# A one-layer hybrid block on one core: h in spaced quarters, a layer norm in single-engine stages, own banks for four transposes, and another buffer for the gate bias

## The chip, the core and the metric

The program runs on one core of a Trainium2 chip. The metric is the time of one execution on the device in microseconds (us), as the median of several runs. Engines are called by their names or, in rows of the profile, by short ones: PE is TensorE (matmuls), PEld its loading of weights, DVE is VectorE, ACT is ScalarE, POOL is GpSimd, SP is SyncE. In this kernel POOL does almost nothing but issue transfers.

## The reference

One decoder layer (DEPTH 1, 256 positions, 2048 channels) with four parallel token mixers of width 1024, all in float32:

```python
h = rmsnorm(x, norm_g)
proj = einsum('bsd,df->bsf', h, w_in)                  # 2048 -> 18432, split into 14 parts
ya = stick_breaking_attention(a_q, a_k, a_v) * silu(a_g)
yb = conformer_conv(b_a, b_b, ...) * silu(b_g)         # GLU, 31-tap causal conv, layernorm over channels, silu
yc = spatial_gating(gelu(c_u), gelu(c_v), ...) * silu(c_g)
yd = dilated_mixture(d_q, d_k, d_v) * silu(d_g)        # 8 heads, 3 dilation groups
yproj = einsum('bsnc,ncd->bsnd', stack(ya, yb, yc, yd), w_branch)
gates = sigmoid(einsum('bsd,df->bsf', h, w_gate) + b_gate)   # one gate per branch and channel
merged = sum over branches of gates * yproj
out = rmsnorm(x + merged @ w_out, final_g)
```

The convolution's layer norm is: subtract the mean over the 1024 channels, divide by the root of the variance, scale and shift per channel, SiLU.

## The kernel before

**Jobs.** All weights stream from memory once, as 256 tiles of 128x2048 (1 MB). Nearly every tile is a job: SyncE loads it (st), ScalarE rounds it to float32r (hi, line 119), VectorE subtracts to get the remainder (lo, line 125), and TensorE multiplies with both parts (hi and lo of the weights against hi and lo of the activations, three products). A table of jobs (prog) is walked in order by run(): before job t's matmuls are issued, the load of job t+5 and the hi and lo of job t+2 are issued; behind the matmuls come the job's own post function and whatever earlier functions asked for with later(n, ...), "n jobs from now". The order of instructions on PE, ACT, DVE and SP is the order in which this Python code issues them; each engine works strictly in that order. GpSimd's order is set by the scheduler. There are three buffers each for hi and lo, six for st.

**Kinds of jobs.** In transposed projections (proj_t, mm_t: lines 261 and 264) the weights are stationary and a job is 16 matmuls of 512 columns and 16 of 256. In the others (mm_n: lines 313 to 315) the activations are stationary and a job is 24 matmuls of 512 columns; four jobs make a column of 512 outputs for two blocks of 128 positions (tb).

**PSUM.** Four pools of two banks: x, n, t and s. A column of mm_n takes the pair n or the pair t in turn (n_banks); a transposed projection takes one bank of t; small products of the mixers take s. The pair x is used for one column in the opening only.

**The stages, in order.** (1) Opening: 16 jobs make the values of d and a from x directly, while the statistics of h are taken (h_squares, h_rms) and h is made and split in four quarters (h_split, lines 241, 88, 89), each of which is four scalings on VectorE, a rounding on ScalarE and a subtraction on VectorE. h_rstd turns the root around for the values' scaling (d_out, a_out). (2) b's projections and its convolution on VectorE, then d's heads; head by head: scores, exponentials, softmax, transposes (pp), product with the values (o). The convolution's layer norm runs among the jobs of d's last two heads. (3) d's gates, b's gate path, branch d; b's gates; a's heads and c's units; gates and branches b, a, c in this manner: a gate column (gate_plain) adds its bias (bgb) on VectorE, ScalarE takes the sigmoid and stores it; a branch column (branch) multiplies the product by the gate (gl, line 491), adds the running sum from memory (ml, line 493) and stores it again. (4) In branch c the merged columns are transposed (turn, pt) and the output projection follows (pso).

**Buffers that the change touches.** The gate bias and the running sum share two buffers (pool sm2_p, tag ml). The values of the mixers (load_v) have one buffer (pool v_p, tag v). Both kinds of tile hold 2 KB in each partition. The bias of a column is loaded when the load of the column's first job is issued, five jobs ahead. In c's units, two mixing products (pz) of c's last two units stand behind the last matmul of c's first gate column; in the same way head 7's last product (o) stands behind that of d's first gate column. For branch b, yl (line 453) is the remainder of the branch's input.

Of the kernel before, what the change touches and what calls it, by code (L numbers as in the profile page):

```python
# [9 lines left out]
F32 = mybir.dt.float32  # L10
F32R = mybir.dt.float32r
AF = mybir.ActivationFunctionType
# [3 lines left out]
P = 128  # L16
# [34 lines left out]
C_K = 272  # L51
# [6 lines left out]
def hybrid_block(ctx: ExitStack, tc, w, x, xT, vec, bg, bgb, cst, dmask, sgu_wT, sgu_lg, sgu_lb, sgu_b, final_g, out):  # L58
    nc = tc.nc
    V, A, T = nc.vector, nc.scalar, nc.tensor  # L60
# [5 lines left out]
    v_p = ctx.enter_context(tc.tile_pool(name="v", bufs=1))  # L66
# [6 lines left out]
    sm2_p = ctx.enter_context(tc.tile_pool(name="ml", bufs=2))  # L73
    sm_p = ctx.enter_context(tc.tile_pool(name="sm", bufs=2))
    dr_p = ctx.enter_context(tc.tile_pool(name="dr", bufs=1, space=bass.MemoryType.DRAM))
    ps_x = ctx.enter_context(tc.tile_pool(name="psx", bufs=2, space=bass.MemoryType.PSUM))
    ps_n = ctx.enter_context(tc.tile_pool(name="psn", bufs=2, space=bass.MemoryType.PSUM))
    ps_t = ctx.enter_context(tc.tile_pool(name="pst", bufs=2, space=bass.MemoryType.PSUM))
# [8 lines left out]
    def split(hi, lo, src):  # L87
        A.activation(hi, src, AF.Copy)  # L88
        V.tensor_sub(lo, src, hi.bitcast(F32))
# [39 lines left out]
    def later(n, fn):  # L129

        t, left = now[0], n
        while left > 0 and t + 1 < len(prog):
            t += 1
            left -= prog[t].size
        calls.setdefault(max(t, now[0] + 1), []).append(fn)
# [8 lines left out]
    def put(job):  # L144
        prog.append(job)
# [25 lines left out]
    cst_sb = cp.tile([P, C_K], F32, name="cst_sb")  # L171
# [10 lines left out]
    def rsqrt(dst, src, n, shape):  # L182

        w = shape[1]
        sc = (so_p.tile([P, 2, w], F32, tag="so", name="rs") if w == S else
              ev_p.tile([P, 2, w], F32, tag=f"rs{w}", bufs=1, name="rs"))
        vp, sq = sc[:, 0, :], sc[:, 1, :]
        V.tensor_scalar(vp, src, 1.0 / n, EPS, op0=ALU.mult, op1=ALU.add)
        A.activation(sq, vp, AF.Sqrt)
        V.reciprocal(dst, sq)  # L190
        if shape[1] == 1:
            V.scalar_tensor_tensor(sq, dst, vp, dst, op0=ALU.mult, op1=ALU.mult)
        else:
            V.tensor_mul(sq, dst, dst)
            V.tensor_mul(sq, sq, vp)
        V.tensor_scalar(sq, sq, -0.5, 1.5, op0=ALU.mult, op1=ALU.add)
        V.tensor_mul(dst, dst, sq)
# [14 lines left out]
    def norm_g(k):  # L212
        return vec_sb[:, V_NG + k:V_NG + k + 1]
# [17 lines left out]
    def h_rms():  # L231
        red = box["red"]
        pst = ps_s.tile([P, 512], F32, tag="s", name="pst")
        T.matmul(pst[:, :S], ones, red[:, 0, :], start=True, stop=False)
        T.matmul(pst[:, :S], ones, red[:, 1, :], start=False, stop=True)
        rsqrt(rstd[:], pst[:, :S], float(D), [P, S])

    def h_split(q):
        for k in range(4 * q, 4 * q + 4):
            xk = xt[k // 8][:, k % 8, :]  # L240
            V.scalar_tensor_tensor(xk, xk, norm_g(k), rstd[:], op0=ALU.mult, op1=ALU.mult)
        ks = slice(4 * q, 4 * q + 4)
        split(xhl[:, ks, 0:S], xhl[:, ks, S:2 * S], xt[q // 2][:, 4 * (q % 2):4 * (q % 2) + 4, :])
# [7 lines left out]
    box = {}  # L251
# [53 lines left out]
    def mm_n(ps, weights, k0, lh, first, last, tbs=(0, 1)):  # L305

        hi, lo = weights
        for kk in range(4):
            o = kk * 512
            for tb in tbs:  # L310
                st = first and kk == 0
                sp = last and kk == 3
                T.matmul(ps[tb][:], lh(k0 + kk, 0, tb), hi[:, o:o + 512], start=st, stop=False)  # L313
                T.matmul(ps[tb][:], lh(k0 + kk, 0, tb), lo[:, o:o + 512], start=False, stop=False)  # L314
                T.matmul(ps[tb][:], lh(k0 + kk, 1, tb), hi[:, o:o + 512], start=False, stop=sp)  # L315

    def n_banks(i, name):

        pool, tag = ((ps_n, "n"), (ps_t, "t"))[i % 2]
        return [pool.tile([P, 512], F32, tag=tag, name=name) for _ in range(2)]  # L320
# [40 lines left out]
    def gate_plain(b, c):  # L361

        bi, acc = BRANCH[b], {}

        def fetch():
            acc["b"] = sm2_p.tile([P, 512], F32, tag="ml", name="bgb")
            o = c * 512
            nc.gpsimd.dma_start(acc["b"][:], bgb[bi, :, o:o + 512].to_broadcast([P, 512]))

        def mm(q):  # L370
            def fn(hi, lo):
                if q == 0:
                    acc["ps"] = n_banks(c, "psg")
                mm_n(acc["ps"], (hi, lo), 4 * q, x_lh, q == 0, q == 3)
            return fn

        def out_g():
            for tb in range(2):
                g = so_p.tile([P, 512], F32, tag="so", name="g")
                V.tensor_add(g[:], acc["ps"][tb][:], acc["b"][:])  # L380
                later(1, lambda tb=tb, g=g: out_s(tb, g))

        def out_s(tb, g):
            A.activation(g[:], g[:], AF.Sigmoid)
            nc.scalar.dma_start(g_dr[bi, tb, :, c * 512:(c + 1) * 512], g[:])
            stored.add((b, c, tb))

        for q in range(4):
            put(Job(("gateN", bi * 4 + c, q), mm(q), keep=(lambda st: fetch()) if q == 0 else None,
                    post=out_g if q == 3 else None))  # L390

    def v_plain(name, func, lh=None, pairs=None, scale=None, jobs=None):

# [36 lines left out]
    def put_y(b, h, n, src):  # L430
        nc.gpsimd.dma_start(y_dr[b][:, h:h + n, :], src)
        stored.update((b, "y", h + k) for k in range(n))
# [75 lines left out]
    def xu_banks(pool, tag):  # L508
        return lambda: [pool.tile([P, 512], F32, tag=tag, name="psv") for _ in range(2)]

    nc.gpsimd.dma_start(vec_sb[:, V_CW:], vec[:, V_CW:])
    d_out = v_plain("d_v", AF.Copy, xu_lh, (xu_banks(ps_n, "n"), xu_banks(ps_x, "x")), True, first_job)
    a_out = v_plain("a_v", AF.Copy, xu_lh, (xu_banks(ps_t, "t"), xu_banks(ps_n, "n")), True)
    at = {0: lambda: nc.sync.dma_start(cst_sb[:], cst[:, 0:C_K]), 3: h_squares, 5: lambda: (h_rms(), h_split(0)),
          6: lambda: h_split(1), 7: lambda: h_split(2), 8: lambda: h_split(3), 9: h_rstd,
          10: lambda: d_out(0), 11: lambda: d_out(1), 12: lambda: a_out(0), 15: lambda: later(1, lambda: a_out(1))}
    for i, fn in at.items():
        prog[i].post = fn

# [100 lines left out]
    def bc8(ap):  # L620
        return ap.unsqueeze(1).to_broadcast([P, KB, S])
# [6 lines left out]
    def chan_sum(red):  # L628
        ps = ps_s.tile([P, 512], F32, tag="s", name="pcs")
        T.matmul(ps[:, 0:S], ones, red[:], start=True, stop=True)  # L630
        return ps
# [6 lines left out]
    def conv_norm2(red):  # L638
        cv = box["cv"]
        pm = chan_sum(red)  # L640
        mean = sm_p.tile([P, S], F32, tag="mean", bufs=1, name="mean")
        A.activation(mean[:], pm[:, 0:S], AF.Copy, scale=1.0 / BW)
        V.tensor_sub(cv[:], cv[:], bc8(mean[:]))
        csq = s_p.tile([P, KB, S], F32, tag="s", name="csq")
        A.activation(csq[:], cv[:], AF.Square)
        later(2, lambda: conv_norm_r(csq))

    def conv_norm_r(csq):
        red = chan_red(csq[:])
        later(2, lambda: conv_norm3(red))  # L650

    def conv_norm3(red):
        cv = box["cv"]
        pv = chan_sum(red)
        rs = sm_p.tile([P, S], F32, tag="mean", bufs=1, name="rs")
        rsqrt(rs[:], pv[:, 0:S], float(BW), [P, S])
        V.tensor_mul(cv[:], cv[:], bc8(rs[:]))
        for i in range(8):
            A.activation(cv[:, i, :], cv[:, i, :], AF.Silu, bias=vec_sb[:, V_LB + i:V_LB + i + 1],
                         scale=vec_sb[:, V_LG + i:V_LG + i + 1])  # L660
        put_y("b", 0, KB, cv[:])

    for h0 in range(0, NH, 2):
# [24 lines left out]
    for c in range(4):  # L688
        gate_plain("d", c)
# [161 lines left out]
    mh, ml, held = [], [], {}  # L851

    def turn(c):
        if c == 0:
            mh.extend(s_p.tile([P, KB, S], F32R, tag="s", name=f"mh{i}") for i in range(2))
            ml.extend(s_p.tile([P, KB, S], F32R, tag="s", name=f"ml{i}") for i in range(2))
        for f0 in (0, 2):
            pt = ps_t.tile([P, 512], F32, tag="t", name="pt")
            for f in range(2):
                for tb in range(2):  # L860
                    o = f * S + tb * P
                    T.transpose(pt[:, o:o + P], held[c, tb][:, (f0 + f) * P:(f0 + f + 1) * P], ident)
            ks = slice(4 * (c % 2) + f0, 4 * (c % 2) + f0 + 2)
            src = pt[:].rearrange("p (f t) -> p f t", f=2)
            A.activation(mh[c // 2][:, ks, :], src, AF.Copy)
            V.tensor_sub(ml[c // 2][:, ks, :], src, mh[c // 2][:, ks, :].bitcast(F32))  # L866
# [46 lines left out]
    acc, wts = {}, {}  # L913
# [99 lines left out]
```

## Time and profile before

| | |
|---|---|
| median of 3 runs | 1512.89 us (1509.95 to 1514.67) |
| the profiled execution, its time | 1509.23 us |
| its span, first to last instruction | 1507.3 us |
| mean granted clock of TensorE | 0.995 |
| weight loads st in one transfer: number, size, median from issue to landing | 254, 1 MB, 4.9 us |
| DMA, mean over the span | 221 GB/s |

A row of the timeline reads: start, duration, engine, line, operation, what it writes and reads, shapes, how many were merged (x4), and in brackets how long the engine had been idle before it and what ended that. A row of a list of waits reads: who waited, for whom, us in total, how many times, the longest. A row of the view of windows reads: the stretch, its length, busy us and number of instructions (in brackets) of PE, PEld, DVE, ACT and POOL, then the granted clock of TensorE (1.00 is full), the busy share of the DMA engines and GB/s.

### The profile page before, as it was taken

How to read it: one execution, taken by the hardware profiler on the slowest of the kernel's cores; microseconds unless marked ns; L12 is line 12 of the kernel's file. 1: busy time of each engine (PE TensorE's matmuls, PEld its weight loads, DVE VectorE, ACT ScalarE, POOL GpSimd, SP SyncE). 2: the span in 40 equal slices, each digit the busy share in tenths (PEclk: the TensorE clock that was granted, in tenths of full speed). 3: DMA queues.
4: the chain of work that ended last, by engine and by line, in shares of the span. 5: the costliest groups of instructions: out<-in, count | busy, mean ns of one | idle time of the engine just before them, and what ended most of it. 6: DMA issues, size and time to landing. Idle time of an engine off the chain costs nothing.

```text
span 1507.3 us, 18226 instructions
## 1 busy us (share of the span) xinstructions
PE 1476.0 (98%) x7428; PEld 1248.4 (83%) x7428; DVE 946.2 (63%) x1080; ACT 704.2 (47%) x657; POOL 94.8 (6%) x174
## 2 busy tenths in 40 slices
PE   7999999999999899999999999999999999999997
PEld 6788888888888788888888888888888888887785
DVE  6848888878888654465444555457565546566554
ACT  6454444444445544353444555547653344344342
POOL 0010000000000000011000000010011101201000
PEclk9999999999999999999999999999999999999999
DMA  8675554554545456777665455577589768888451
GB/s 328 239 267 187 194 184 160 182 189 168 210 168 182 165 187 241 255 269 277 238 228 200 166 185 184 186 276 266 188 281 314 273 234 289 292 293 273 162 192 56
DMA packets 58340, 332.63 MB, mean 221 GB/s; under 512 B 7728, under 2 KB 7856, under 8 KB 24848
## 3 DMA queue, kind: packets, MB, share of 16 engines
q1 hardware_dynamic: 38880, 271.74, 50.4%
q0 software_dynamic: 14048, 50.29, 9.9%
q10 hardware_dynamic: 5328, 9.45, 1.7%
q8 instruction: 58, 0.95, 0.3%
q14 instruction: 26, 0.21, 0.0%
HBM read 305.23 MB, written 26.21 MB: 220 GB/s over the span
## 4 chain that ended last, share of the span: by engine, by line
PE 88%; DVE 5%; DMA 3%; ACT 2%; issue 1%; POOL 0%; DVEq 0%; ACTq 0%
PE ps L261 29%; PE ps L264 14%; PE psg L314 7%; PE psg L315 7%; PE psg L313 7%; PE psy L313 3%; PE psy L315 3%; PE psy L314 3%; DMA ml<-m_dr 2%; PE psv L314 2%; PE psv L315 2%; PE pso L314 2%; PE pso L315 2%; PE pso L313 2%; PE psv L313 2%; DVE lo L125 2%
## 5 line engine op out<-in xcount | busy, mean ns | idle before, releaser
L125 DVE TENSOR_TENSOR lo<-st,hi 128x2048 fp32r<-128x2048 f32 x248 | 566.9, 2289 | 375.9 <-ACT hi L119 366.0
L261 PE MATMUL ps<-xhl,hi 128*128 128x512 f32 x1920 | 682.4, 401 | 4.7 <-DVE dst L294 4.3
L119 ACT ACTIVATE hi<-st 128x2048 fp32r<-128x2048 f32 x248 | 473.5, 1911 | 323.3 <-PE psg L315 181.4
L264 PE MATMUL ps<-xhl,lo 128*128 128x256 f32 x1920 | 519.5, 281 | 0.0
L261 PEld LDWEIGHTS ps<-xhl,hi 128*128 128x128 f32 x1920 | 357.3, 189 | 83.0 <-DVE dst L294 4.6
L264 PEld LDWEIGHTS ps<-xhl,lo 128*128 128x128 f32 x1920 | 363.5, 189 | 9.3
L314 PE MATMUL psg<-lo,xhl 128*128 128x512 f32 x512 | 199.4, 390 | 1.2 <-DVE lo L125 1.2
L313 PE MATMUL psg<-hi,xhl 128*128 128x512 f32 x512 | 199.8, 390 | 0.0
L315 PE MATMUL psg<-hi,xhl 128*128 128x512 f32 x512 | 199.2, 389 | 0.0
L293 ACT ACTIVATE bt<-ps 128x256 f32<-128x256 f32 x120 | 45.9, 383 | 318.2 <-PE ps L261 309.9
L532 DVE SCALAR_TENSOR_TENSOR cv<-glu,vec_sb,cv 128x255 f32<-128x255 f32 (+14 forms) x240 | 112.3, 468 | 6.6
L314 PEld LDWEIGHTS psg<-lo,xhl 128*128 128x128 f32 x512 | 96.1, 188 | 21.9 <-DVE lo L125 2.1
L315 PEld LDWEIGHTS psg<-hi,xhl 128*128 128x128 f32 x512 | 96.1, 188 | 20.1
L313 PEld LDWEIGHTS psg<-hi,xhl 128*128 128x128 f32 x512 | 96.1, 188 | 19.6
L313 PE MATMUL psy<-hi,yh 128*128 128x512 f32 x256 | 100.6, 393 | 1.9 <-DVE ml L866 1.9
L314 PE MATMUL psy<-lo,yh 128*128 128x512 f32 x256 | 100.3, 392 | 0.0
L315 PE MATMUL psy<-hi,yl 128*128 128x512 f32 x256 | 100.2, 391 | 0.0
L294 DVE TENSOR_TENSOR dst<-ps,bt 128x256 f32<-128x256 f32 x120 | 50.6, 421 | 78.6 <-ACT bt L293 75.4
L313 PE MATMUL psv<-hi,xuh 128*128 128x512 f32 x128 | 51.6, 403 | 7.6 <-ACT hi L88 7.6
L313 PEld LDWEIGHTS psy<-hi,yh 128*128 128x128 f32 x256 | 48.3, 189 | 12.0 <-DVE ml L866 2.1
L315 PEld LDWEIGHTS psy<-hi,yl 128*128 128x128 f32 x256 | 48.5, 189 | 10.3
L314 PEld LDWEIGHTS psy<-lo,yh 128*128 128x128 f32 x256 | 48.5, 189 | 10.1
(211 smaller groups left out, 1192.4 us busy)
## 6 DMA issues: line engine op xcount, KB each, us to landing
st<-in_w_dram SPq DMA_DIRECT2D x254, 1024.0 KB, 4.9
g_dr<-g ACTq DMA_DIRECT2D x32, 256.0 KB, 5.3
gl<-g_dr POOLq DMA_DIRECT2D x32, 256.0 KB, 6.0
m_dr<-gl POOLq DMA_DIRECT2D x24, 256.0 KB, 6.1
ml<-m_dr POOLq DMA_DIRECT2D x24, 256.0 KB, 5.4
bgb<-in_bgb_dram POOLq DMA_DIRECT2D x16, 256.0 KB, 4.0
xr<-in_x_dram POOLq DMA_DIRECT2D x8, 256.0 KB, 4.8
xt<-in_xT_dram SPq DMA_DIRECT2D x3, 512.0 KB, 11.0
```

Source lines behind the costliest of these rows:

```text
L119: A.activation(self.hl[0], self.st[:], AF.Copy)
L125: V.tensor_sub(self.hl[1], self.st[:], self.hl[0].bitcast(F32))
L261: T.matmul(ps[:], hi[:, o:o + P], rhs[:, k, :], start=start, stop=stop)
L264: T.matmul(ps[:, 0:S], lo[:, o:o + P], rhs[:, k, 0:S], start=False, stop=False)
L293: A.activation(bt[:], ps[:, S:2 * S], AF.Copy)
L294: V.tensor_add(dst[:, j, :], ps[:, 0:S], bt[:])
L313: T.matmul(ps[tb][:], lh(k0 + kk, 0, tb), hi[:, o:o + 512], start=st, stop=False)
L314: T.matmul(ps[tb][:], lh(k0 + kk, 0, tb), lo[:, o:o + 512], start=False, stop=False)
L315: T.matmul(ps[tb][:], lh(k0 + kk, 1, tb), hi[:, o:o + 512], start=False, stop=sp)
L532: V.scalar_tensor_tensor(dst, src, wc, dst, op0=ALU.mult, op1=ALU.add)
```

## The change

It has four parts.

1. **Opening.** The statistics' matmuls and the root (h_rms) come one job later, and the quarters of h behind jobs 7, 9, 11 and 13 instead of 5, 6, 7 and 8. The root's turn (h_rstd) and the scalings of the values move into the jobs between.
2. **Layer norm.** The stages that issued work on two engines at once are cut: subtraction of the mean; one job later the squares on ScalarE; one later their sum over channels; one later the root; one later the scaling on VectorE; one later four SiLUs; one later the other four and the store. The root comes one job earlier than before, the scaling behind the same job, the SiLUs one and two jobs later.
3. **Transposes of the merged columns** take the pair x instead of the pair t.
4. **Gate bias** takes the values' buffer (v) instead of one of the two of the running sum, and its load is issued in the program at the column's second job instead of five jobs ahead of the first.

```diff
@@ gate_plain
-            acc["b"] = sm2_p.tile([P, 512], F32, tag="ml", name="bgb")
+            acc["b"] = v_p.tile([P, 512], F32, tag="v", name="bgb")
...
             def fn(hi, lo):
+                if q == 1:
+                    fetch()
                 if q == 0:
...
-            put(Job(("gateN", bi * 4 + c, q), mm(q), keep=(lambda st: fetch()) if q == 0 else None,
-                    post=out_g if q == 3 else None))
+            put(Job(("gateN", bi * 4 + c, q), mm(q), post=out_g if q == 3 else None))
@@ opening
-    at = {0: ..., 3: h_squares, 5: lambda: (h_rms(), h_split(0)),
-          6: lambda: h_split(1), 7: lambda: h_split(2), 8: lambda: h_split(3), 9: h_rstd,
-          10: lambda: d_out(0), 11: lambda: d_out(1), 12: lambda: a_out(0), 15: lambda: later(1, lambda: a_out(1))}
+    at = {0: ..., 3: h_squares, 6: h_rms, 7: lambda: h_split(0),
+          8: h_rstd, 9: lambda: (h_split(1), d_out(0)), 10: lambda: d_out(1), 11: lambda: h_split(2),
+          12: lambda: a_out(0), 13: lambda: h_split(3),
+          15: lambda: later(1, lambda: a_out(1))}
@@ layer norm of the convolution
         V.tensor_sub(cv[:], cv[:], bc8(mean[:]))
+        later(1, conv_norm_s)
+
+    def conv_norm_s():
         csq = s_p.tile([P, KB, S], F32, tag="s", name="csq")
-        A.activation(csq[:], cv[:], AF.Square)
-        later(2, lambda: conv_norm_r(csq))
+        A.activation(csq[:], box["cv"][:], AF.Square)
+        later(1, lambda: conv_norm_r(csq))
 
     def conv_norm_r(csq):
         red = chan_red(csq[:])
-        later(2, lambda: conv_norm3(red))
+        later(1, lambda: conv_norm3(red))
...
         rsqrt(rs[:], pv[:, 0:S], float(BW), [P, S])
-        V.tensor_mul(cv[:], cv[:], bc8(rs[:]))
-        for i in range(8):
+        later(1, lambda: conv_norm4(rs))
+
+    def conv_norm4(rs):
+        V.tensor_mul(box["cv"][:], box["cv"][:], bc8(rs[:]))
+        later(1, conv_norm5)
+
+    def conv_norm5(i0=0):
+        cv = box["cv"]
+        for i in range(i0, i0 + 4):
             A.activation(cv[:, i, :], cv[:, i, :], AF.Silu, ...)
+        if i0 == 0:
+            later(1, lambda: conv_norm5(4))
+            return
         put_y("b", 0, KB, cv[:])
@@ turn
-            pt = ps_t.tile([P, 512], F32, tag="t", name="pt")
+            pt = ps_x.tile([P, 512], F32, tag="x", name="pt")
```

More of the change, by code (lines that the diff above doesn't have):

```diff
@@ L513, in hybrid_block @@
     a_out = v_plain("a_v", AF.Copy, xu_lh, (xu_banks(ps_t, "t"), xu_banks(ps_n, "n")), True)
-    at = {0: lambda: nc.sync.dma_start(cst_sb[:], cst[:, 0:C_K]), 3: h_squares, 5: lambda: (h_rms(), h_split(0)),
-          6: lambda: h_split(1), 7: lambda: h_split(2), 8: lambda: h_split(3), 9: h_rstd,
-          10: lambda: d_out(0), 11: lambda: d_out(1), 12: lambda: a_out(0), 15: lambda: later(1, lambda: a_out(1))}
+    at = {0: lambda: nc.sync.dma_start(cst_sb[:], cst[:, 0:C_K]), 3: h_squares, 6: h_rms, 7: lambda: h_split(0),
+          8: h_rstd, 9: lambda: (h_split(1), d_out(0)), 10: lambda: d_out(1), 11: lambda: h_split(2),
+          12: lambda: a_out(0), 13: lambda: h_split(3),
+          15: lambda: later(1, lambda: a_out(1))}
     for i, fn in at.items():
@@ L643, in conv_norm2 @@
         V.tensor_sub(cv[:], cv[:], bc8(mean[:]))
+        later(1, conv_norm_s)
+    def conv_norm_s():
         csq = s_p.tile([P, KB, S], F32, tag="s", name="csq")
-        A.activation(csq[:], cv[:], AF.Square)
-        later(2, lambda: conv_norm_r(csq))
+        A.activation(csq[:], box["cv"][:], AF.Square)
+        later(1, lambda: conv_norm_r(csq))
     def conv_norm_r(csq):
         red = chan_red(csq[:])
-        later(2, lambda: conv_norm3(red))
+        later(1, lambda: conv_norm3(red))
     def conv_norm3(red):
-        cv = box["cv"]
         pv = chan_sum(red)
```

## The prediction

> **What bounds the kernel now.** I read the page's busy table first, then the list of waits for TensorE, then the places that the list names, engine by engine, and last the granted clock around them.
>
> ```profile
> PE 1476.0 (98%) x7428; PEld 1248.4 (83%) x7428; DVE 946.2 (63%) x1080; ACT 704.2 (47%) x657; POOL 94.8 (6%) x174
> ```
>
> TensorE is busy for 98% of the span, so only what opens or closes a gap on it moves the end. The list of its waits (engine, line, what it waited for: us in total, times, longest) gives the gaps:
>
> ```profile
> PE ps L261 <- DVE dst L294: 4.3, 1, 4.3
> PE psv L314 <- DVE lo L125: 2.7, 4, 1.1
> PE psy L313 <- DVE ml L866: 1.9, 1, 1.9
> PE pt L862 <- DVE gl L491: 1.3, 2, 0.7
> PE psg L314 <- DVE lo L125: 1.2, 2, 0.8
> ```
>
> These five lines are in four places: the opening (psv), the convolution's layer norm (ps), the last branch (psy, pt), and the merging of the branches (psg). An idle stretch starts at a modelled end, and a 512-column matmul is drawn 0.39 us long while the next one starts 0.23 after it, so each wait costs about 0.16 more than its idle time. The clock adds to two of them. In this view of windows (PE busy first, the granted clock after the five engines) the first row follows the ps gap, the second holds the psy gap and the third follows it:
>
> ```profile
> 511.11:517.93 6.82, 5.52 (x17) 4.75 (x18) 3.26 (x9) 4.75 (x8) 0.00 (x0) 0.50 0.52 192
> 1391.75:1395.16 3.41, 1.53 (x7) 1.23 (x7) 3.28 (x5) 2.55 (x3) 1.60 (x3) 1.00 0.99 386
> 1395.17:1398.57 3.40, 3.40 (x9) 2.67 (x8) 1.45 (x1) 0.00 (x0) 0.53 (x1) 0.50 0.47 148
> ```
>
> At half clock the 5.52 us of the first row that are busy lose 2.8, and the 3.40 of the third 1.7. All that can be had is the gaps and these 4.5 us, some 18 of 1507.
>
> **The opening (h in quarters).** VectorE's cycle per job, and TensorE's last wait there:
>
> ```profile
> 57.23 1.67 DVE L241 SCALAR_TENSOR_TENSOR xt<-xt,vec_sb,rstd 128x256 f32<-128x256 f32 x4
> 64.04 1.67 DVE L241 SCALAR_TENSOR_TENSOR xt<-xt,vec_sb,rstd 128x256 f32<-128x256 f32 x4
> 77.79 0.50 PE L314 MATMUL psv<-lo,xuh 128*128 128x512 f32 x1 [1.09 <-DVE lo L125]
> 57.00:78.00 21.00, 18.25 (x78) 14.01 (x78) 15.88 (x21) 10.56 (x8) 0.54 (x1) 1.00 0.52 179
> 78.00:104.00 26.00, 26.00 (x116) 21.49 (x116) 13.46 (x6) 12.89 (x11) 3.98 (x7) 1.00 0.84 313
> ```
>
> With one quarter of h in each job the cycle is 6.81 us (64.04 less 57.23). From 78 on TensorE does 116 matmuls in 26 us, 0.224 each, so its job of 24 takes 5.4, and the 78 matmuls of the window before should have taken 17.5 instead of 21: 3.5 us lost. The change puts a job without a quarter between two that have one. On VectorE the order there, difference of the two programs (xt, xhl: scaling and splitting a quarter; lo: a job's weights):
>
> ```order
>  L197 TENSOR_TENSOR rstd<-rstd,rs 128x256
> +L125 TENSOR_TENSOR lo<-st,hi 128x2048
>  L241 SCALAR_TENSOR_TENSOR xt_116<-xt_116,vec_sb,rstd 128x256 x4
>  L89 TENSOR_TENSOR xhl<-xt_116,xhl 128x4x256
>  L125 TENSOR_TENSOR lo<-st,hi 128x2048
> +L249 COPY rstd_n<-psn 128x2
> +L125 TENSOR_TENSOR lo<-st,hi 128x2048
> ```
>
> Two jobs (10.9 us of TensorE) now hold one cycle of 6.81 and one lo of 2.3, 9.1 in all. My replay of every job from 6 to 15 leaves each lo 2.6 us or more ahead of its use, and the last quarter ready at about 92, where its first reader (job 16) starts at about 100. The statistics' two matmuls move one job later and cost what they cost now. Bounds: 0 (another wait takes the place) and 3.5. I take **-3.5**, since the sum of VectorE's work fits.
>
> **Layer norm in stages.** What stands there now (the first two rows, from the chain, give the pitch of a job of this kind, 5.65):
>
> ```profile
> 116.13 0.47 PE ps L261 x2
> 121.78 0.47 PE ps L261 x2
> ...
> 491.80 2.29 DVE L125 TENSOR_TENSOR lo<-st,hi 128x2048 fp32r<-128x2048 f32 x1
> 498.01 1.28 ACT L659 ACT_TABLE_LOAD   x1
> 498.03 1.75 DVE L190 RECIPROCAL rs<-rs 128x256 f32<-128x256 f32 x1 [0.97 <-ACT rs L189]
> 501.52 2.29 DVE L657 TENSOR_TENSOR cv<-cv,rs 128x2048 f32<-128x2048 f32 x1
> 503.85 4.05 ACT L659 ACTIVATE cv<-cv,vec_sb 128x256 f32<-128x256 f32 x8 [4.55 <-DVE cv L657]
> 507.80 1.89 ACT L119 ACTIVATE hi<-st 128x2048 fp32r<-128x2048 f32 x1
> 512.41 0.80 PE L261 MATMUL ps<-xhl,hi 128*128 128x512 f32 x1 [4.28 <-DVE dst L294]
> 513.34 0.61 ACT L579 ACTIVATE ph_d<-ph_d,sm 128x384 f32<-128x384 f32 x1 [2.07 <-DVE sm L577]
> 514.87 1.89 ACT L119 ACTIVATE hi<-st 128x2048 fp32r<-128x2048 f32 x1
> 519.33 0.16 DVE L584 RECIPROCAL sm<-sm 128x2 f32<-128x2 f32 x1
> 521.16 0.35 DVE L588 TENSOR_SCALAR ph_d<-ph_d,sm 128x256 f32<-128x256 f32 x1
> 521.28 0.27 PE L594 MATMUL pp<-cst_sb,ph_d 128*128 128x128 f32 x1
> ```
>
> ScalarE waits 4.55 us for VectorE's scaling, does eight SiLUs, and only then rounds the hi of the job that TensorE starts at 512.41 instead of 508.0: a gap of 4.4 and 2.8 of clock. The transposes of head 7's softmax (pp) come at 521.28 instead of 508.0 + 5.65 + 0.45 for two score products = 514.1, and wait another 0.3 among themselves: 7.5 lost. Now ScalarE's order, before and then after (rs: the norm's square root; ph_d: head 7's exponentials; cv: SiLUs):
>
> ```order
> L189 ACTIVATE rs<-rs 128x256
> L659 ACT_TABLE_LOAD
> L659 ACTIVATE cv<-cv,vec_sb 128x256 x8
> L119 ACTIVATE hi<-st 128x2048
> L293 ACTIVATE bt<-ps 128x256
> ```
>
> ```order
> L189 ACTIVATE rs<-rs 128x256
> L119 ACTIVATE hi<-st 128x2048
> L293 ACTIVATE bt<-ps 128x256
> L119 ACTIVATE hi<-st 128x2048
> L293 ACTIVATE bt<-ps 128x256
> L581 ACT_TABLE_LOAD
> L581 ACTIVATE ph_d_901,sm<-ph_d_901,sm 128x384
> L581 ACTIVATE ph_d_902,sm<-ph_d_902,sm 128x768
> L670 ACT_TABLE_LOAD
> L670 ACTIVATE cv<-cv,vec_sb 128x256 x4
> L119 ACTIVATE hi<-st 128x2048
> ```
>
> Two hi have moved ahead of the SiLUs, so the job at 508.0 finds its weights. But the first four SiLUs now stand behind head 7's exponentials and ahead of the next hi. Replayed on VectorE: the root's chain starts at 491.8, one job earlier than now, and takes 4.4 (3.49 from the reciprocal's start to the scaling at 501.52, 0.9 before it); then, in its order, lo 2.2, an addition 0.3, the scaling 2.2, lo 2.2, an addition 0.3 and head 7's scores with their maxima 1.0: 504.5. On ScalarE: exponentials 1.5 (513.34 to 514.87), table 1.3, four SiLUs 2.0 (half of 4.05), hi 1.9: 511.3. Then lo 2.2 and one addition: 513.9. Softmax 2.2 (519.33 to 521.51): 516.1, and only then can the second transpose go. TensorE gets there at 514.1, so a new gap of **2.1** (two pieces, about 0.9 and 1.1) replaces the old one. Its bounds are 0 and the old 4.4. Clock: the window of 3.41 us above with 1.53 busy, 1.88 idle, was followed by half clock; whether one window catches both new pieces is about an even chance, so I take 0.85, between 0 and 1.7. Net 7.5 - 2.1 - 0.85 = **-4.55**.
>
> The Trainium skill ("TensorE: Matmul & The Clock Gate", the closing table of what matters for kernels) warns only of gaps over about 3 us, one whole idle window. The trace doesn't agree: 1.88 idle of 3.41 sufficed at 1391.75. By the rule the new gap would cost no clock and the sum would be 0.85 better.
>
> **Own banks for the transposes.** In the last branch:
>
> ```profile
> 1379.36 0.66 PE L862 MATMUL pt<-cst_sb,gl 128*128 128x128 f32 x4 [0.67 <-DVE gl L491]
> 1390.78 1.03 PE L862 MATMUL pt<-cst_sb,gl 128*128 128x128 f32 x8
> 1393.69 0.50 PE L313 MATMUL psy<-hi,yh 128*128 128x512 f32 x1 [1.88 <-DVE ml L866]
> ```
>
> The transposes share two banks with columns 1 and 3: after column 1 and after column 3 they wait for the multiplication out of those banks (1.3 idle in two waits, about 2.2 with the drawn overlap and the late first start), after column 2 column 3 waits for the transposes' readers (1.88, so 2.04). The other pair was last used in the opening, so all three vanish, and the half clock after the third with it: 2.2 + 2.04 + 1.7 = **-5.9**. Next in line there is lo, which VectorE has done a job ahead. Bounds: 0 and 5.9; nothing else claims the pair.
>
> **Gate bias in the values' buffer.** The bias no longer takes one of the two buffers of the running sum (ml). Now:
>
> ```profile
> ml<-m_dr POOLq DMA_DIRECT2D x24, 256.0 KB, 5.4
> 1183.58 0.54 POOL L475 DMA_DIRECT2D ml<-m_dr  x1 [6.37 <-DVE gl L493]
> 1189.19 0.69 DVE L493 TENSOR_TENSOR gl<-gl,ml 128x512 f32<-128x512 f32 x1 [5.31 <-DMA ml<-m_dr]
> ```
>
> The load could be issued only when the first half's addition had freed its buffer, VectorE stood 5.31 us for it, and TensorE twice waited for the lo behind that (the psg line: 1.2 + 2 x 0.16). With both buffers free a column ahead (10.9 us; a load lands in 5.4, the first row) this goes: **-1.55**. In exchange there is one buffer for bias and values. Of sixteen columns, fourteen follow another bias, whose buffer comes free some 20 us before use. Two follow the values: d's first column waits for head 7's last product, c's first for the last two mixing products, both issued on TensorE behind that column's last matmul. POOL, difference told by before and then after, around c's first column (xr: the residual; y_dr_c: stores):
>
> ```order
> L893 DMA xr<-in_x_dram 128x512 x2
> L475 DMA ml<-m_dr 128x512
> L431 DMA y_dr_c<-dst 128x256 x2
> L893 DMA xr<-in_x_dram 128x512 x2
> L472 DMA gl<-g_dr 128x512 x3
> ```
>
> ```order
> L907 DMA xr<-in_x_dram 128x512 x2
> L368 DMA bgb<-in_bgb_dram 128x512 x2
> L432 DMA y_dr_c<-dst 128x256 x2
> L907 DMA xr<-in_x_dram 128x512 x2
> L473 DMA gl<-g_dr 128x512 x3
> ```
>
> The bias takes the place of an ml load, and what is behind it (stores of c, the residual) isn't due for 100 us. What it costs on VectorE:
>
> ```profile
> 564.03 0.72 POOL L427 DMA_DIRECT2D v<-v_dr_a_v  x1 [55.29 <-PE o L604]
> DMA to landing us min/median/max: 3.3/4.0/7.2
> 1113.43 1.37 DVE L380 TENSOR_TENSOR g<-psg,bgb 128x512 f32<-128x512 f32 x2 [0.52 <-PE psg L315]
> 1113.91 1.05 PE L826 MATMUL pz<-swb,v 128*128 128x128 f32 x8
> 1117.21 2.28 DVE L453 TENSOR_TENSOR yl<-yf,yh 128x2048 fp32r<-128x2048 f32 x1
> ```
>
> (The second row is the bias loads'.) At c: mixing 1113.91 to 1114.7, issue 0.55 later, landing 4.0 after: 1119.3. From there VectorE does what it now does from 1113.43: additions and mixing 3.8, yl 2.2, lo 2.3, done at 1127.6. That lo's job starts at 1114.7 + 10.9 = 1125.6 and needs it at 1125.8: a gap of **+1.85**, or 1.15 to 5.05 with the shortest and longest landing. At d the same issue (564.03) lands at 568.0; without the mixing and yl the lo is done at 572.1, due at 574.6: nothing, at most 0.7.
>
> **Sum.** -3.5 - 4.55 - 5.9 - 1.55 + 1.85 = -13.65. The profiled execution took 1509.23, which gives 1495.6; it lies 3.66 below the median of the runs, 1512.89, and from that the sum gives **1499.2**.
>
> **Rivals.** (1) The bias lands late in c's column: 7.2 instead of 4.0 adds 3.2, and a gap of 5 us draws a half-clock window, 1.7: 1504.1. For it speaks that the queues are 50 to 99% busy in the windows above; against it that 4.0 is the median of sixteen. (2) The norm leaves no gap at all, because head 7's scores come earlier than I replayed: 2.95 less, 1496.3. (3) By the skill's rule the half clock at 1395.17 isn't due to the psy gap and stays, while the new gap draws none: +1.7 - 0.85, 1500.1; against it, it starts within 2 us of the gap. (4) The own banks free nothing, as the next column then waits for VectorE itself: +5.9, 1505.1; against it, lo is a job ahead there. (5) Slower: the single bias buffer makes every column late. POOL works in order, and the row at 564.03 shows it standing 55 us for one buffer. VectorE can be held about 7 us past a column's end before TensorE stops; beyond that each column pays in full. If POOL stood so long that fourteen columns each paid 2 us, 28 more than forecast, it would be 1527; it decides from 1 us a column. Against it: the bias is first in its stretch of the queue, some 20 us before use.
>
> **How the numbers follow.** My forecast 0.55; rivals in their order 0.15, 0.15, 0.05, 0.07, 0.03. The range 1492 to 1507 holds the forecast, (1) to (4), a d-gap of 0.7, and the spread between the profile's base and the median's. 0.3% of 1512.89 is 4.5 us, about what a measurement can tell from no change; 1508.4 is passed only by (5) and by (1) with (4) together: faster 0.91, same 0.06, slower 0.03.
>
> **What would show it.** Right: no psv wait for lo after 50 us; the wait at 512 gone, a shorter one at pp about 2 us long; no wait of pt or psy for VectorE; VectorE's waits for ml near 0; a psg wait of 1 to 2 us for lo in c's second column, and VectorE's addition waiting about 5 us for bgb in two columns. Wrong: a psg wait in many columns, or half clock for more than two windows after the start.

## The result, and the profile after

| | before | after |
|---|---|---|
| median of the runs of this comparison | 1511.42 us (1509.34 to 1514.67) | 1489.86 us (1489.80 to 1490.15) |
| the profiled execution, its time | 1509.23 us | 1490.15 us |
| its span | 1507.3 us | 1488.3 us |
| mean granted clock in it | 0.995 | 0.998 |

The changed kernel takes 0.9856 of the time before, 95% interval 0.9836 to 0.9876: 21.6 us less, where 13.65 less was forecast. The time lies below the range.

The busy table and then the list of waits of the changed kernel (TensorE's first wait is the start of the program, as is 6.4 us of it before):

```profile
PE 1468.0 (99%) x7428; PEld 1245.0 (84%) x7428; DVE 945.6 (64%) x1080; ACT 704.9 (47%) x658; POOL 95.4 (6%) x174
```

```profile
PE psv L313 <- ACT hi L88: 6.6, 1, 6.6
PE psg L314 <- DVE lo L125: 1.0, 1, 1.0
PE pp L597 <- DVE ph_d L590: 0.9, 1, 0.9
PE pso L314 <- DVE hi L89: 0.7, 1, 0.7
PE psv L314 <- DVE lo L89: 0.4, 1, 0.4
...
DVE g L382 <- DMA bgb<-in_bgb_dram: 11.7, 2, 5.9
```

The psv waits for lo of line 125, the wait at ps of 4.3 and the waits of psy and pt for VectorE are gone. The two waits that the prediction expected as new ones are there: pp, and psg in one place. VectorE waits twice for bgb. Its waits for ml have shrunk from six to one; the rows of the two lists of waits, before and then after:

```profile
DVE gl L493 <- DMA ml<-m_dr: 22.6, 6, 5.3
DVE gl L494 <- DMA ml<-m_dr: 2.1, 1, 2.1
```

TensorE's work has not changed (7428 matmuls).

Where on TensorE the 19.0 us of the two spans came from is seen by the start of the first matmul of each kind (ps: transposed projections; psg: gates; psy: branches; pso: output). The last column is the prediction's term.

| stretch on TensorE | before, us | after, us | difference | forecast |
|---|---|---|---|---|
| start of the span to first ps | 104.90 | 98.10 | -6.80 | -3.5 |
| to first psg (b, d's heads, norm) | 435.17 | 429.54 | -5.63 | -4.55 |
| to the first gate column of c | 551.97 | 552.11 | +0.14 | 0 |
| c's gates, to first psy of branch b | 44.53 | 45.86 | +1.33 | +1.85 |
| branches b and a with gates | 219.44 | 217.60 | -1.84 | -1.55 |
| branch c, to first pso | 52.37 | 46.17 | -6.20 | -5.9 |
| output, to the end | 98.92 | 98.92 | 0 | 0 |

Every term has its sign and place; the opening is off by 3.3, the norm by 1.1, the rest by about half a microsecond or less.

**The opening** gained in two places. The stretch in which the quarters are made runs without a gap in the view of windows (TensorE busy 51.60 of 51.60 us; before, 18.25 of 21.00 in the worst part of it):

```profile
52.40:104.00 51.60, 51.60 (x238) 42.74 (x237) 34.61 (x33) 24.45 (x20) 4.55 (x8) 1.00 0.67 233
```

But there is a difference much earlier, before any quarter is made. The timeline of the kernel before (rows of POOL, ACT and PE):

```profile
2.03 1.07 POOL L368 DMA_DIRECT2D bgb<-in_bgb_dram  x2
14.66 0.91 ACT L217 ACTIVATE xuh<-xt,vec_sb 128x256 fp32r<-128x256 f32 x2 [1.89 <-DMA xt<-in_xT_dram]
16.57 0.49 PE L313 MATMUL psv<-hi,xuh 128*128 128x512 f32 x1 [1.18 <-ACT hi L88]
17.83 0.50 PE L314 MATMUL psv<-lo,xuh 128*128 128x512 f32 x1 [0.77 <-DVE lo L89]
```

and of the changed kernel, where POOL issues nothing behind the first of these rows for the rest of the opening's first 20 us:

```profile
1.36 0.67 POOL L512 DMA_DIRECT2D vec_sb<-in_vec_dram  x1 [0.45 <-issue]
11.73 0.91 ACT L217 ACTIVATE xuh<-xt,vec_sb 128x256 fp32r<-128x256 f32 x2 [1.69 <-DMA xt<-in_xT_dram]
14.90 0.50 PE L314 MATMUL psv<-lo,xuh 128*128 128x512 f32 x1 [0.42 <-DVE lo L89]
```

At 2.03 us the kernel before issues two bias loads of 256 KB whose first user, the first gate column, starts at 540: their two buffers were free and POOL had nothing to wait for ahead of them. (The program asks for a bias five jobs ahead, as the text on the buffers says; in the trace, where the scheduler sets GpSimd's order, these two loads stand 540 us ahead.) ScalarE's start on the tile of x that it waits for comes 2.9 us later with them (14.66 against 11.73), and TensorE's wait for lo ends 2.93 later (17.83 against 14.90). Of the 6.80, 2.93 are of this place; the other 3.87 come behind it, in the stretch with the quarters.

**The norm.** Rows of the changed kernel's timeline, ScalarE, VectorE, TensorE:

```profile
497.62 0.62 ACT L581 ACTIVATE ph_d<-ph_d,sm 128x384 f32<-128x384 f32 x1 [0.66 <-DVE sm L579]
...
499.27 1.28 ACT L670 ACT_TABLE_LOAD   x1
500.56 2.08 ACT L670 ACTIVATE cv<-cv,vec_sb 128x256 f32<-128x256 f32 x4
502.55 1.90 ACT L119 ACTIVATE hi<-st 128x2048 fp32r<-128x2048 f32 x1
...
504.48 2.29 DVE L125 TENSOR_TENSOR lo<-st,hi 128x2048 fp32r<-128x2048 f32 x1 [6.89 <-ACT hi L119]
...
508.84 0.35 DVE L590 TENSOR_SCALAR ph_d<-ph_d,sm 128x256 f32<-128x256 f32 x1
...
509.34 0.30 PE L597 MATMUL pp<-cst_sb,ph_d 128*128 128x128 f32 x1 [0.88 <-DVE ph_d L590]
```

It is the chain that was forecast, link by link: exponentials, table, four SiLUs, hi, lo (VectorE has waited 6.89 for that hi), softmax, second transpose. The gap on TensorE is 0.88 of idle. By the starts of the products it costs 1.8 with the short wait at the scores just ahead (2.90 us from the last ps before the scores to the first behind the transposes; 1.13 in the experiment below in which there is no wait). No half clock follows.

**c's gate columns.** Rows of POOL, VectorE and TensorE after the change:

```profile
1101.62 1.05 PE L840 MATMUL pz<-swb,v 128*128 128x128 f32 x8
1102.97 0.54 POOL L368 DMA_DIRECT2D bgb<-in_bgb_dram  x1 [15.31 <-PE pz L840]
1106.56 1.29 DVE L382 TENSOR_TENSOR g<-psg,bgb 128x512 f32<-128x512 f32 x2 [5.94 <-DMA bgb<-in_bgb_dram]
...
1112.46 6.69 DVE L125 TENSOR_TENSOR lo<-st,hi 128x2048 fp32r<-128x2048 f32 x3
1114.80 0.50 PE L314 MATMUL psg<-lo,xhl 128*128 128x512 f32 x1 [1.01 <-DVE lo L125]
```

The bias is issued behind the last mixing product and VectorE's addition starts 3.6 us after the issue (4.0 was taken); the lo behind it is late by 1.01 of idle.

### The profile page after: what moved, and what is told of

It is laid out like the page before. It is cut to its first block, busy times and chain, and to the rows that moved or that the text cites. A ratio compares the mean times of both kernels' runs of the same rounds, so it can differ in the third digit from the quotient of the medians.

```text
span 1488.3 us, 18226 instructions
## 1 busy us (share of the span) xinstructions
PE 1468.0 (99%) x7428; PEld 1245.0 (84%) x7428; DVE 945.6 (64%) x1080; ACT 704.9 (47%) x658; POOL 95.4 (6%) x174
## 4 chain that ended last, share of the span: by engine, by line
PE 94%; DVE 3%; ACT 2%; DMA 1%; issue 1%; DVEq 0%; ACTq 0%
PE ps L261 28%; PE ps L264 14%; PE psg L314 8%; PE psg L315 8%; PE psg L313 8%; PE psy L315 4%; PE psy L313 4%; PE psy L314 4%; PE psv L314 3%; PE psv L315 3%; PE psv L313 3%; PE pso L314 2%; PE pso L315 2%; PE pso L313 2%; DVE lo L125 1%
```

## The experiments

Each experiment is an edit of the changed kernel, timed against it by the median (1489.86) and beside runs of the kernel before, 1510.27 (1507.82 to 1511.67) for the first four experiments and 1510.39 (1508.04 to 1514.19) for the others. Ratios are to the kernel before. Four undo one part each; they say what that part is worth where the other three stand. The changed kernel was not run again beside them, and the medians of the kernel before differ by 1.2 us between the three groups of runs. So a difference of one to two microseconds, as in the last experiments, is read in the profile first, and the time only has to agree.

**The opening of before alone.** The table that says behind which job each step comes is put back.

```diff
-    at = {..., 3: h_squares, 6: h_rms, 7: lambda: h_split(0), 8: h_rstd,
-          9: lambda: (h_split(1), d_out(0)), 10: lambda: d_out(1), 11: lambda: h_split(2),
-          12: lambda: a_out(0), 13: lambda: h_split(3), 15: ...}
+    at = {..., 3: h_squares, 5: lambda: (h_rms(), h_split(0)), 6: lambda: h_split(1), 7: lambda: h_split(2),
+          8: lambda: h_split(3), 9: h_rstd, 10: lambda: d_out(0), 11: lambda: d_out(1), 12: lambda: a_out(0), 15: ...}
```

> The changed kernel with the opening's order as before (a quarter of h behind each of jobs 5 to 8). Theory A, VectorE's cycle of 6.8 us per job is what stopped TensorE there: four waits for lo between 55 and 80 us come back, the span is 3.5 to 3.8 us longer than the changed kernel's 1488.3, time about 1493.5. Rival B, the opening got shorter only because transfers came earlier: no such waits, time within 0.5 us of 1489.9.

Measured 1494.14 us (1493.92 to 1494.26), ratio 0.9895 [0.988, 0.991]: 4.28 more than the changed kernel. Its list of waits has the four waits for lo back:

```profile
PE psv L314 <- DVE lo L125: 2.7, 4, 1.1
```

The first ps starts at 102.05 against 98.10, while ScalarE's start on that tile of x (11.80) is as early as in the changed kernel. So the quarters two jobs apart are worth about 4 us, and the other 2.9 us of the opening's gain are not theirs.

**The norm of before alone.**

```diff
     def conv_norm2(...):
-        later(1, conv_norm_s)
         csq = s_p.tile(...)
         A.activation(csq[:], cv[:], AF.Square)
-        later(1, lambda: conv_norm_r(csq))
+        later(2, lambda: conv_norm_r(csq))
...
-        later(1, lambda: conv_norm3(red))
+        later(2, lambda: conv_norm3(red))
...
         V.tensor_mul(cv[:], cv[:], bc8(rs[:]))
-        ... (scaling, SiLUs 0 to 3, SiLUs 4 to 7 in jobs of their own)
+        for i in range(8): A.activation(cv[:, i, :], ..., AF.Silu, ...)
```

> The changed kernel with the convolution's layer norm as before. Theory A: the eight SiLUs ahead of a hi open the gap of 4.4 us again, and half clock follows it; the gap of 1.4 us at the transposes goes, net 4.5 to 6.1 more, time 1494.5 to 1496. The time varies from run to run by up to 1.7 us, as the clock's windows fall differently on the gap. Rival B: the staging only exchanged one gap for another of the same cost, time within 1 us of 1489.9.

Measured 1495.75 us (1495.64 to 1495.88), ratio 0.9906 [0.9891, 0.9921]: 5.89 more. Two rows of its list of waits, then two of its view of windows:

```profile
PE ps L261 <- DVE dst L294: 4.3, 1, 4.3
...
PE pp L597 <- DVE ph_d L590: 0.9, 1, 0.9
```

```profile
500.90:505.30 4.40, 0.41 (x3) 0.10 (x1) 2.39 (x2) 3.53 (x4) 0.54 (x1) 1.00 0.58 238
505.80:509.20 3.40, 3.40 (x11) 2.82 (x11) 0.62 (x4) 2.67 (x5) 0.00 (x0) 0.51 0.83 296
```

The gap of 4.3 and half clock behind it are back; here the half clock lasts one window of 3.4 us, so 1.7, where before it was 6.82. Against the expectation the wait of pp did not go: in this order too, with eight SiLUs ahead of a hi, the softmax comes late. The kernel before shows no such wait in its list; its longer half clock held TensorE back there, which would fit that the stretch from first ps to first psg is almost the same in both, 435.17 and 435.06. The stages on one engine are worth 5.9.

**The transposes in the old banks.**

```diff
-            pt = ps_x.tile([P, 512], F32, tag="x", name="pt")
+            pt = ps_t.tile([P, 512], F32, tag="t", name="pt")
```

> The changed kernel with the transposes of the merged columns in the pair of banks they had before. Theory A: three gaps of 1.1, 2.0 and 1.1 us return, 4.2 in all, time 1494.1; where the middle one falls in one clock window, another 1.7 us of half clock, 1495.8, and that from run to run. Rival B, the clock rule of gaps over 3 us alone: 1494.1 in every run and no half clock after the start.

Measured 1494.6 us (1494.28 to 1496.4), ratio 0.9898 [0.9881, 0.9914]: 4.74 more. In the changed kernel all eight transposes of a column stand in one piece, with no wait ahead of them (timeline, PE):

```profile
1364.97 1.03 PE L876 MATMUL pt<-cst_sb,gl 128*128 128x128 f32 x8
1376.78 1.03 PE L876 MATMUL pt<-cst_sb,gl 128*128 128x128 f32 x8
```

With the old banks the waits are the old ones, here in the list of waits, and the windows show the clock behind the second:

```profile
PE psy L313 <- DVE ml L880: 1.9, 1, 1.9
PE pt L876 <- DVE gl L492: 1.3, 2, 0.7
```

```profile
1378.90:1381.50 2.60, 0.72 (x5) 0.46 (x3) 2.56 (x5) 2.60 (x3) 1.61 (x3) 1.00 0.97 405
1381.60:1385.00 3.40, 3.40 (x10) 2.66 (x9) 2.29 (x1) 0.01 (x1) 0.54 (x1) 0.50 0.49 184
1385.10:1388.50 3.40, 3.40 (x17) 2.77 (x16) 0.00 (x0) 0.10 (x1) 0.00 (x0) 1.00 0.85 306
```

In the windows at 1381.60 and 1385.10 TensorE is busy for all 3.40 us, with 10 matmuls in the one and 17 in the other. This is the profiled execution, the run of 1496.4, with a mean clock of 0.996. The other three took 1494.28, 1494.4 and 1494.8 at 0.998. They have no profile, but by clock and time the same gap brought half clock in one run of four, at about the price of one window (1.7). The banks are worth 4.4 to 4.9 without it and 6.5 with it; in the execution on which the prediction was built the window was there.

**The bias in the buffers of the running sum again.** The buffer and the early load of before are put back.

```diff
-            acc["b"] = v_p.tile([P, 512], F32, tag="v", name="bgb")
+            acc["b"] = sm2_p.tile([P, 512], F32, tag="ml", name="bgb")
...
-                if q == 1:
-                    fetch()
...
-            put(Job(("gateN", bi * 4 + c, q), mm(q), post=...))
+            put(Job(("gateN", bi * 4 + c, q), mm(q), keep=(lambda st: fetch()) if q == 0 else None, post=...))
```

> The changed kernel with the gate bias as before (in the running sum's two buffers, loaded as early as a buffer is free). Theory A: the two bias loads issued at 2 us are back and take transfer time from the first weights and x, so that TensorE's waits in its first 20 us grow by 2 to 3 us; the two waits for lo behind the running sum's load return (1.6 us), the one of 1.2 us in c's gates goes: time about 1493. Rival B, the shorter start of the changed kernel was chance: only 1.6 - 1.2 us, time 1490.3.

Measured 1495.88 us (1495.7 to 1497.01), ratio 0.9908 [0.9894, 0.9923]: 6.02 more, about 3 more than expected. Its list of waits, VectorE's wait for ml in the timeline, and the opening in the view of windows:

```profile
PE psv L313 <- ACT hi L88: 8.4, 2, 6.8
...
PE psg L314 <- DVE lo L125: 2.4, 2, 1.4
```

```profile
1182.73 0.69 DVE L493 TENSOR_TENSOR gl<-gl,ml 128x512 f32<-128x512 f32 x1 [5.29 <-DMA ml<-m_dr]
```

```profile
17.10:23.90 6.80, 6.21 (x15) 4.86 (x16) 6.17 (x10) 5.57 (x11) 0.00 (x0) 0.50 1.02 427
```

c's gap is gone (1.33 back), and branches b and a with gates take 3.05 us more, with the two waits of psg in them. The part that I had put at +0.3 in all (-1.55 + 1.85) is worth -6.0. The missing piece is at the start: the bias loads are at 2.03 us again, the second psv wait of hi is back, and half clock stands in the opening from 17.1 to 23.9. In the profiled execution, the run of 1497.01, the first ps is 5.67 late.

**Two early loads, and nothing else.** To see whether the start is the loads' doing, two transfers of the same size and kind are issued at the same point into the buffers of ml; nothing reads what they bring.

```diff
     nc.gpsimd.dma_start(vec_sb[:, V_CW:], vec[:, V_CW:])
+    for i in range(2):
+        nc.gpsimd.dma_start(sm2_p.tile([P, 512], F32, tag="ml", name="early")[:],
+                            bgb[0, :, i * 512:(i + 1) * 512].to_broadcast([P, 512]))
```

> The changed kernel with two loads of the size of a bias, read by nothing, issued by GpSimd at about 2 us, where the kernel before issued its first two bias loads. Theory A: they delay the first x and weights by 2 to 3 us, TensorE waits again around 15 us, and the clock may drop behind that for 3.4 to 6.8 us: time 1492 to 1495. Rival B, the old bias cost its 6 us later, in the merging of the branches: time within 0.5 us of 1489.9.

Measured 1492.53 us (1491.75 to 1493.71), ratio 0.988 [0.9862, 0.9898]: 2.67 more. Timeline and windows of the profiled execution, the one of 1493.71:

```profile
2.03 1.07 POOL L514 DMA_DIRECT2D early<-in_bgb_dram  x2
13.84 0.91 ACT L217 ACTIVATE xuh<-xt,vec_sb 128x256 fp32r<-128x256 f32 x2 [1.94 <-DMA xt<-in_xT_dram]
17.01 0.50 PE L314 MATMUL psv<-lo,xuh 128*128 128x512 f32 x1 [0.76 <-DVE lo L89]
```

```profile
18.20:21.50 3.30, 3.30 (x10) 2.55 (x9) 2.88 (x5) 2.55 (x5) 0.00 (x0) 0.50 1.03 429
```

The same x tile is 2.1 us late (13.84 against 11.73), TensorE's wait ends 2.11 late, and a half-clock window of 3.3 us adds 1.65: the first ps starts at 101.81 instead of 98.10. The two loads near the head of GpSimd's queue cost 1.9 to 3.9 us by run, 2.67 in the median. ScalarE's row above starts at 11.33 to 11.80 in all seven profiles of programs without such loads, and at 13.84 to 14.66 in the three with them, so the delay is not chance. With this, the part of the bias should be 2.67 + 3.05 - 1.33 = 4.4, where 6.0 was measured. The two profiles put the difference into the opening: the first ps is 5.67 late there and 3.71 here, with 6.8 us of half clock there and 3.3 here, so most of it is one more window (1.7). Why the old buffering drew that window, and whether the runs without a profile had it, stays open.

**A second buffer for values and bias.** This takes away the wait that the change brought in.

```diff
-    v_p = ctx.enter_context(tc.tile_pool(name="v", bufs=1))
+    v_p = ctx.enter_context(tc.tile_pool(name="v", bufs=2))
```

> The changed kernel with two buffers for the values and the bias. Theory A: VectorE no longer waits for the bias in d's and c's first columns, TensorE's wait of 1.2 us for the lo in c's gates goes: 1488.7. Rival B: the wait in c is due to VectorE's own backlog (additions, mixing, yl), and only shrinks: over 1489.3.

Measured 1488.44 us (1488.15 to 1488.64), ratio 0.9853 [0.9832, 0.9874]: 1.42 less than the changed kernel. The addition of c's first gate column no longer waits for its bias (timeline, VectorE), and the psg line is gone from the list of waits:

```profile
1100.68 1.37 DVE L382 TENSOR_TENSOR g<-psg,bgb 128x512 f32<-128x512 f32 x2 [0.52 <-PE psg L315]
```

The stretch of c's gates takes 44.54 us, as before the change (44.53). So the +1.33 there is the single buffer's.

**The first four SiLUs one job later.**

```diff
     def conv_norm4(rs):
         V.tensor_mul(box["cv"][:], box["cv"][:], bc8(rs[:]))
-        later(1, conv_norm5)
+        later(2, conv_norm5)
```

> The changed kernel with both halves of the SiLUs one job later. Theory A: the table load and four SiLUs between head 7's exponentials and the next hi are what makes its softmax late for the transposes; the gap there (1.5 us) goes, time 1488.4. Rival B: they now delay the hi of the next job in the same way, time within 0.5 us of 1489.9.

Measured 1488.53 us (1488.18 to 1491.11), ratio 0.9857 [0.9837, 0.9876]: 1.33 less. One of the four runs is 2.6 above the others, at a mean clock of 0.997, and has no profile. The timeline has the hi ahead of the SiLUs now, and both transposes without a wait:

```profile
499.11 1.90 ACT L119 ACTIVATE hi<-st 128x2048 fp32r<-128x2048 f32 x1
503.18 2.08 ACT L670 ACTIVATE cv<-cv,vec_sb 128x256 f32<-128x256 f32 x4
507.44 0.27 PE L596 MATMUL pp<-cst_sb,ph_d 128*128 128x128 f32 x1
507.55 0.27 PE L597 MATMUL pp<-cst_sb,ph_d 128*128 128x128 f32 x1
```

The four SiLUs ahead of that hi were the cause of the gap at pp in the changed kernel. It cost 1.3 us by the medians and 1.8 by the stretch from first ps to first psg (427.77 against 429.54).

**Both, as the better version.** The last two edits together.

> Both of these, two buffers and the SiLUs one job later. Theory A: the two gaps are far apart, so both go: 1489.9 - 1.2 - 1.5 = 1487.2. Rival B: 1488.4 or more, if one of them isn't a gap of its own.

Measured 1486.65 us (1486.37 to 1487.28), ratio 0.9841 [0.9823, 0.9859]: 3.21 less than the changed kernel. The two added are 2.75; the 0.5 between is no more than the four runs spread (0.9). All that TensorE still waits for in it, the program's start aside, is 1.4 us:

```profile
PE psv L313 <- ACT hi L88: 6.8, 1, 6.8
PE pso L314 <- DVE hi L89: 0.7, 1, 0.7
PE ps L261 <- DVE g L382: 0.4, 2, 0.2
PE cc L762 <- DVE pr_a L753: 0.3, 1, 0.3
```

The four reversals add to 4.28 + 5.89 + 4.74 + 6.02 = 20.9, where the change is worth 21.6 in its own comparison and 20.5 from the median of all runs of the kernel before (1510.3). So the parts are nearly independent.

## Why the prediction was wrong, and where it was right

**Wrong: the fourth part's loads.** The prediction followed the bias of c's and d's first columns and the ml loads, but not the first two bias loads, which the same part takes away from the first rows of GpSimd's queue. It put this term at nothing without a reason. The new program issues them only behind the column's second job and when the values' buffer is free. The traces of the two kernels differ in this in POOL's first rows; the prediction quoted and costed only those around c's first column. The term should have been about -2.9 in this execution (2.67 in the two loads' own experiment). It is the largest piece by which the sum on the profiled executions fell short: 19.1 in time against 13.65.

**Wrong: the base.** "It lies 3.66 below the median of the runs, ... and from that the sum gives 1499.2": that carried a spread of the kernel before over to the changed one. The kernel before varies from 1507.82 to 1514.67 over 18 runs, with 1510.3 as their median, so the three runs' 1512.89 was itself 2.6 high. And its time follows its clock: of the runs beside the experiments those at 0.996 took 1507.82, 1508.04 and 1510.72, the one at 0.992 took 1514.19. So what varies is, by these clocks, the time at half clock; that a gap brings it in some runs and not in others is inferred, as most of these runs have no profile. With most gaps closed the changed kernel took 1489.80 to 1490.15 in its four runs, all at 0.998. Nothing had to be added for it: 1495.6 was the place to stop. With the missed 2.9 that is 1492.7, and the norm's 1.1 and the quarters' 0.4 are most of what is left to 1490.15. Of the 9.3 us between 1499.2 and 1489.86 the base is thus the largest piece (3.66), the missed loads the second (2.9).

**Mis-sized: the norm.** -4.55 was forecast, -5.63 came. The new gap was put at 2.1 in two pieces and measured 1.8 in two, 0.3 at the scores and 1.5 at the transposes. The even chance of a half-clock window, 0.85, was not paid, and that is most of the difference. Mechanism and chain were as replayed, and the experiment with the later SiLUs confirms its cause. Rival (2), no gap at all, did not happen.

**Right, within about 0.5 us in the profiled executions:** the quarters (-3.5 forecast; 3.87 in the timeline, 4.28 by the reversal); the own banks (-5.9; -6.20 in the profiled executions, 4.74 by the median of the reversal, since the half clock comes in some runs only); the running sum's loads (-1.55; -1.84); c's bias (+1.85; +1.33, 1.42 by the second buffer); d's bias (0; +0.14).

**The rivals.** (1) The late bias: the load landed in 3.6 us, not 7.2. (3) The half clock behind the psy gap was due to that gap: it is gone with the own banks, and back in one run with the old ones. The Trainium skill ("TensorE: Matmul & The Clock Gate", the closing table) warns only of gaps of over about 3 us. The traces do not agree: 1.88 us sufficed in that run and, by the mean clocks, did not in three others. My own reading, that such a gap always costs a window, doesn't hold either; the cost is a matter of the run. (4) The next column did not wait for VectorE; nothing was behind the banks. (5) No column but c's second paid for the single buffer on TensorE. POOL's waits ahead of bias loads grew, from 164.7 us to 260.6, and cost TensorE nothing more.

## What to carry to other kernels

Where a load moves to another buffer or another place, follow every instance of it, the first ones above all: a load whose buffer is free at the start may be issued there, and then competes with what the first products wait for. Build the forecast on one profiled execution and leave it there: where a kernel's runs spread with their granted clock, as here, the spread may be part of what the gaps cost, and need not be carried over to a kernel without them. When a long operation on one engine is cut into stages, the first piece still has to be placed behind the work that somebody waits for next, which here was worth another 1.3 us.

## What the runs showed of the hardware that was not expected

- Two loads of 256 KB each, issued at 2.03 us into a stretch in which the DMA engines are busy nearly all the time (share 0.95 from 2 to 12 us in the experiment with two early loads, 1.03 in its row at 18.20), delay the tiles of x and weights by 2.1 to 2.9 us. TensorE has two short waits there (1.1 to 1.6 and 0.8 us). No half clock stands behind them in the kernel before (1.00 from 12.8 to 57 us), but one window of it in that experiment, and 6.8 us in the one with the old bias.
- A gap of 1.88 us on TensorE drew half clock in one run of four (the three others by their mean clock alone), for one window of 3.4 us with 10 matmuls in it instead of 17. Gaps of 0.9 to 1.0 us drew none in the profile of the changed kernel. A gap of 4.3 us drew 6.82 us of half clock in the kernel before and 3.4 in the experiment with the old norm.
